# Overflow branch moved in front of the last portion of the expert stream, and the output step behind it in two engines' hands

## Chip, cores and metric

The kernel runs on one core of one Trainium2 chip. The metric is the device time of one launch in microseconds (us); the median of the runs counts.

## What is computed

Two layers of a diffusion backbone over 256 latent tokens and 256 context tokens, 1024 wide. The end of layer 2 is what this change touches: a mixture of eight experts, two per token, then a norm, a gate and the residual.

```python
def moe_swiglu(y, w_r, b_r, wg, wu, wd):
    logits = (y @ w_r).astype(jnp.float32) + b_r.astype(jnp.float32)
    top_val, top_idx = lax.top_k(logits, TOP_K)
    gates = jax.nn.softmax(top_val, axis=-1)
...
    for e in range(N_EXPERTS):
        out = out + combine[..., e:e + 1] * swiglu(y, wg[e], wu[e], wd[e])
    return out
# in the layer:
f = ffn(modulate(rmsnorm(h, g_ffn_pre[i]), sh_f, sc_f))
h = h + gt_f * rmsnorm(f, g_ffn_post[i])
```

## The kernel before

The order of the work is written out while the kernel is built: tasks are Python generators, a planner (`Sched`) picks the next step by estimated times, and each engine gets its instructions in that fixed order. Line 310 is the helper that emits every operation, so nearly all rows carry L310.

The experts' weights, 2 MB each (128 partitions by 4096 floats), come through one queue, SP's, in `t_load` (line 517). Each goes into one of eight big buffers, named `w` in the trace, and a buffer is reused when its last reader is done. An expert's hidden width of 3584 is cut into seven blocks; a block has two transfers for gate and up and one for down, so 6 MB. `moe_items` lists the transfers: block n's gate and up, then block n-1's down.

Tokens are gathered per unit of work. Unit 0 is a fixed expert's, units 1 to 7 are the others by falling load, with room for 160, 96, 96, 64, 64, 64 and 32 tokens (`SLOTS`). `SEQ` gives the order as (unit, first block, block behind the last); its last three entries are unit 7's blocks 2 and 3, then all seven blocks of unit 3 (96 tokens), then unit 7's blocks 4 to 6. `experts` spawns for each entry the gate and up products (`t_xgu`), the down products (`t_xdown`) and the finish (`t_xfinish`: ACT and DVE split the sum in a high and a low part, TensorE spreads it back to the tokens, and DVE adds it to `facc`, the sum over experts, with the token's weight).

Tokens that find no room in their unit go to up to five overflow units, computed only if needed: `moe_over` loads the number of them (`novf`) into a register of every engine, and a nest of five `tc.If` blocks holds the overflow work. That work streams its weights through the same eight buffers, splits them there (ACT and DVE) and multiplies them (TensorE). Each engine runs its own branch when it comes to it in its own order. On the side not taken, each engine waits until its own semaphore (for SP: the eight semaphores of its transfers) has reached the count of everything issued so far, adds what the skipped work would have added, and jumps over the overflow work. The input of these runs has no overflow.

In the kernel before, everything but the last finish comes ahead of the branch. Behind it come that finish (`self.last`) and `fin`: ACT squares `facc` with a running sum, DVE multiplies both token halves (t = 0, 1) by the gate, computes the reciprocal root in ten small operations, and scales and adds the residual in four half tiles, each sent out by SP. `t_gate` builds the gate tile from two groups of TensorE transposes and ACT copies; it waits for a block three before the end of the last entry of `SEQ`.

Of the kernel before, what the change touches and what calls it, by code (L numbers as in the profile page):

```python
# [16 lines left out]
F32 = mybir.dt.float32  # L17
# [4 lines left out]
OP = mybir.AluOpType  # L22
# [4 lines left out]
NE = 8  # L27
FF = 3584
FC = FF // 128
EB = FF // 512  # L30
# [14 lines left out]
MORE = 5  # L45
# [23 lines left out]
POB, HIB = (-1.5, -0.3, -0.8), -0.5  # L69
# [10 lines left out]
PE, ACT, DVE, POOL, DMA, NONE = "PE", "ACT", "DVE", "POOL", "DMA", "NONE"  # L80


def on(eng, *res, ev=()):

    return eng, res, tuple(ev)
# [295 lines left out]
class Core:  # L381
# [196 lines left out]
    def stream(self, items):  # L578


        items = [it if len(it) == 4 else (*it, 1) for it in items]
        for kind, key, ap, n in items:
            for k in [(*key, j) for j in range(4)] if kind[0] == "b" else [key]:
                self.raw[k], self.piece[k], self.uses[k] = Event(), Event(), n
        items = [it[:3] for it in items]
        self.sc.spawn(self.t_load(items))
        self.sc.spawn(self.t_hi(items), HIB)

    def g_proj(self, p, key, c0, c1, kk=2, more=None):

# [1042 lines left out]
        rest = slots - n  # L1633
        return [(s, None) for s in range(0, n, 128)] + ([(n, [64] * (rest // 64) + [32] * (rest % 64 // 32))] if rest else [])

    def experts(self, units, seq):

        go = self.sc.spawn
        prev, state, near = None, {}, []
        for key, b0, b1 in seq:  # L1640
            _, pos, base, slots, comb = units[key]
            down = []
            parts = self.parts(slots)
            for s, ws in parts:
                if b0 == 0:
                    out, hts = [[Event(), Event()], [Event() for _ in ws or [128]]], [Event() for _ in range(EB)]
                    ev = near if prev is None else [*near, *prev] if key >= NE else [*near, *prev, self.combed]
                    go(self.t_xgather(key, pos, base + s, ws, out, ev) if ws else self.t_gather(key, pos, base + s, [out[0], out[1][0]], ev), -0.3)
                    prev = out[0]
                    state[key, s] = out, hts  # L1650
                out, hts = state[key, s]
                if key in JOIN and b0:
                    continue
                d1 = EB if key in JOIN else b1
                acc = [Event() for _ in ws or [128]]
                down.append((self.t_xdown(key, b0, d1, ws, hts, acc) if ws else self.t_edown(key, b0, d1, hts, acc[0]), 0.0))
                for i, w in enumerate(ws or [128]):
                    finish, a = self.t_xfinish if ws else self.t_finish, (comb, acc[i], out[1][i], d1 == EB, *([w] if ws else []))
                    if (key, b0, b1) == seq[-1] and key < NE and (s, ws) == parts[-1] and i == len(ws or [128]) - 1:

                        self.last = lambda done, f=finish, a=a: f(*a, done)
                    else:
                        down.append((finish(*a), -0.2))
            for b in range(b0, b1):
                for s, ws in reversed(parts):
                    out, hts = state[key, s]
                    go(self.t_xgu(key, b, ws, out[0], hts[b]) if ws else self.t_egu(key, b, out[0], hts[b]))
            if self.facc is None:
                self.facc = []
                go(self.t_facc([hts[3]]))  # L1670
            if key not in JOIN:
                near = [hts[max(b0, b1 - NEAR)]]
            if (key, b0, b1) == seq[-1] and key < NE:
                go(self.t_gate([self.colev[1, 5], hts[max(b0, b1 - 3)]]))
            for t in down:
                go(*t)

# [122 lines left out]

    def moe_over(self):

        tc, nc = self.tc, self.nc
        self.sc.settle(KEEP, 3)
        novf = nc.values_load(self.onum[0:1, MORE:MORE + 1], min_val=0, max_val=MORE)
        oidx = [nc.values_load(self.onum[0:1, i:i + 1], engines=(mybir.EngineType.SP,), min_val=0, max_val=NE - 1)
                for i in range(MORE)]

        def more(i):
            with tc.If(novf > i, preferred_fallthrough_block=False):  # L1810
                key = NE + i
                self.stream(self.moe_items([(key, 0, EB)], oidx[i]))
                self.experts({key: (key, lambda: self.otab[:, i, 0:2], 128, 128, lambda: self.otab[:, i, 2:4])}, [(key, 0, EB)])
                self.sc.run()
                if i < MORE - 1:
                    more(i + 1)

        more(0)


    @staticmethod
# [37 lines left out]
    def items(self):  # L1859
        a = self.a  # L1860
        win = lambda i, cs: [("w", ("in", i, c), a["w_in"][i, c]) for c in cs]
        wout = lambda i, s: [("w", ("out", i, s, c), a["w_out"][i, c]) for c in self.wout_order(i, s)]
        ada = lambda i, ch: [("ada", ("ada", i, ch, k), a["w_ada"][i, ch, k]) for k in range(KC)]
        dft = lambda i: [("w", ("dft", i), a["dft"], 2)]
        rest = lambda n: [("rest", None, n)]

        def mix(ws, xs):

            out, n = [], 0
            for j, w in enumerate(ws):  # L1870
                out.append(w)
                m = len(xs) * (j + 1) // len(ws)
                out += xs[n:m]
                n = m
            return out

        x = [("x", t, a["x" if t < 2 else "ctx"][(t % 2) * 128:(t % 2) * 128 + 128, :]) for t in range(4)]
        first = ada(0, 0) + ada(0, 1)
        it = rest(0)
        first[8:8] = win(0, ORD[0][:NW])  # L1880
        for i, w in enumerate(first):
            it += [x[XP.index(i)]] if i in XP else []
            it.append(w)
        m = max(NW, 3)
        it += win(0, ORD[0][NW:m]) + mix(win(0, ORD[0][m:]) + dft(0) + wout(0, 0), mix(sum([ada(0, ch) for ch in (3, 4, 2) if ch not in PA], []), sum([ada(0, ch) for ch in PA], []))) + wout(0, 1)
        ffn = []
        for f in range(FC + 1):
            if f < FC:
                n = 2 if f < NSPLIT else 1
                ffn += [("w", ("gate", f), a["w_gate_d"][f], n), ("w", ("up", f), a["w_up_d"][f], n)]  # L1890
            if f > 0:
                ffn += [("w", ("down", 0, f - 1), a["w_down_d"][f - 1])]
        it += mix(ffn, ada(0, 5) + ada(1, 0) + ada(1, 1) + ada(1, 3) + ada(1, 4))
        it += mix([("w", ("down", 1, f), a["w_down_d"][f]) for f in range(FC)], ada(1, 2) + ada(1, 5))
        it += win(1, ORD[1]) + dft(1)
        moe = self.moe_items(self.seq())
        it += rest(REST1) + moe[:KW] + wout(1, 0) + moe[KW:]
        return it

# [11 lines left out]
    def body(self):  # L1911
        nc, a = self.nc, self.a
# [27 lines left out]
        go = sc.spawn  # L1940
        sc.clock[DMA] = DC
        sc.spawn(self.main())
        sc.run()
        self.moe_over()
        self.fin()

    def main(self):
        go = self.sc.spawn
# [82 lines left out]
        self.sc.rest = REST[0]  # L2031
        self.sc.change, self.sc.stay = CHG, STAY
        tab = lambda u, c: self.tab[:, c:c + 2, 0] if u == 0 else self.utab[:, c:c + 2, u - 1]
        self.experts({u: (u, lambda u=u: tab(u, 0), 0, self.slots(u), lambda u=u: tab(u, 2)) for u in range(NE)}, self.seq())

    def fin(self):

        done = [[Event(), Event()] for _ in range(2)]
        ss = self.fixed([128, 8], F32, "ss", 4)

        def squares():
            junk = yield on(ACT, "h")
# [4 lines left out]
                    self.s.activation(junk, self.facc[t][:, hf * 512:hf * 512 + 512], AF.Square, scale=1.0 / 32.0, accum_out=ss[:, i:i + 1])  # L2047
            self.sc.rel(junk)

        def out(sq):  # L2050
            o = []
            for t in range(2):
                o.append((yield on(DVE, "k", ev=done[t])))
                self.v.tensor_mul(o[t], self.facc[t], self.gate[1, 5, 0].v)
            yield on(DVE, ev=[sq])
            x, t, y = self.fixed([128, 4], F32, "rx", 2), self.fixed([128, 4], F32, "rt", 2), self.fixed([128, 4], F32, "ry", 6)
            self.v.scalar_tensor_tensor(x[:, :2], ss[:, 0:4:2], EPS, ss[:, 1:4:2], op0=OP.add, op1=OP.add)
            self.rsqrt(y[:, :2], x[:, :2], t[:, :2])
            for t in range(2):
                for hf in range(2):  # L2060
                    c = slice(hf * 512, hf * 512 + 512)
                    self.v.scalar_tensor_tensor(o[t][:, c], o[t][:, c], y[:, t:t + 1], self.h[t][:, c], op0=OP.mult, op1=OP.add)
                    self.nc.sync.dma_start(self.out[t * 128:t * 128 + 128, c], o[t][:, c])

        self.sc.spawn(self.last(done))
        self.sc.spawn(out(self.sc.spawn(squares())))
        self.sc.run()


_NAMES = ["x", "ctx", "cc", "consts", "consts2", "dft", "w_ada", "b_ada", "b_cols", "g_cols", "g_mix_post", "g_ffn_post", "w_in",  # L2070
# [98 lines left out]
```

## Time and profile before

| what | us |
|---|---|
| median of 3 runs | 1666.61 (1664.62 to 1667.5) |
| profiled execution | 1667.74 |
| its span, first to last instruction | 1666.0 |
| TensorE busy (matmul) | 1593.7 (96%) |
| DVE, ACT, Pool busy | 786.0, 528.9, 26.1 |

The profile is of one execution. A span of 1666.0 us leaves 1.74 us of its time outside the instructions; this execution was 1.13 us above the median. Times of rows count from the start of the span. PE is TensorE's matmuls, PEld its weight loads, SPq the instructions of SP's queue. Matmuls are pipelined, so a PE that is busy all the time is not a PE at its peak.

### The profile page before, as it was taken

Reading aid. Unit: us, or ns where it says so; the run is one execution under the profiler, and the core shown is the slowest. Engines: PE = TensorE matmul, PEld = TensorE weight load, DVE = VectorE, ACT = ScalarE, POOL = GpSimd, SP = SyncE. Lnnn points to the kernel's source line nnn. Section 1 sums busy time; section 2 is a strip of 40 time slices with the busy share of each in tenths; the row PEclk is TensorE's granted clock in tenths of the full one; section 3 lists DMA queues with packets and bytes.
Section 4 is the critical chain, followed back from the end, with each engine's and each line's share of the span. In section 5 each row is a group of like instructions: output and inputs, shape, how many; then the busy total and the mean of one; then the engine's idle time right before and its main releaser. Section 6 shows DMA issues by size and latency. Waiting matters only on the chain. (4 is left out here: it accounts for less than half of the span.)

```text
span 1666.0 us, 25796 instructions
## 1 busy us (share of the span) xinstructions
PE 1593.7 (96%) x10596; PEld 1029.8 (62%) x10596; DVE 786.0 (47%) x1479; ACT 528.9 (32%) x952; POOL 26.1 (2%) x49
## 2 busy tenths in 40 slices
PE   5999999999999999999998999999999999999995
PEld 3776789888888888897655544444454443343333
DVE  4576688765644448897643342342352421021004
ACT  3477354232322225566613232132132200000001
POOL 0100000000000001000000000000000000000000
PEclk9999999999999999999988999999999999999998
DMA  9515444645554556784499999999999999999994
GB/s 374 214 39 228 164 152 165 214 144 180 170 167 156 174 168 227 259 330 155 152 344 418 421 427 427 426 426 397 427 391 419 427 426 425 425 426 426 426 422 181
DMA packets 71758, 497.30 MB, mean 299 GB/s; under 512 B 9004, under 2 KB 9136, under 8 KB 52048
## 3 DMA queue, kind: packets, MB, share of 16 engines
q1 hardware_dynamic: 68976, 490.76, 74.6%
q0 software_dynamic: 1792, 4.18, 0.8%
q8 instruction: 85, 1.39, 0.3%
q10 hardware_dynamic: 864, 0.62, 0.1%
q14 instruction: 41, 0.34, 0.1%
HBM read 494.49 MB, written 1.05 MB: 297 GB/s over the span
## 5 line engine op out<-in xcount | busy, mean ns | idle before, releaser
L310 PE MATMUL b<-s,s 128*128 128x512 f32 (+2 forms) x2864 | 580.5, 364 | 7.9 <-DVE s L310 6.8
L310 PEld LDWEIGHTS b<-s,s 128*128 128x128 f32 (+1 forms) x2864 | 460.6, 187 | 96.5 <-issue 9.6
L310 PE MATMUL b<-w,f 128*32 128x256 f32 (+1 forms) x2336 | 293.5, 468 | 5.7 <-DMA w<-in_w_gu_e_dram 5.7
L310 PE MATMUL b<-w,s 128*32 128x256 f32 (+2 forms) x1848 | 272.4, 437 | 3.1 <-DMA w<-in_w_gu_e_dram 2.7
L310 DVE TENSOR_TENSOR f<-f,b 128x256 f32<-128x256 f32 (+2 forms) x105 | 41.1, 393 | 480.8 <-ACT f L310 372.3
L310 ACT ACTIVATE f<-b 128x512 f32<-128x512 f32 (+4 forms) x188 | 85.6, 460 | 567.1 <-PE b L310 563.2
L310 PE MATMUL b<-s,f 128*32 128x256 f32 (+1 forms) x1344 | 208.3, 405 | 19.0 <-DVE ones L782 8.6
L310 ACT ACTIVATE s<-s 128x1024 fp32r<-128x1024 f32 (+2 forms) x173 | 179.0, 1050 | 147.2 <-PE b L310 84.0
L310 PEld LDWEIGHTS b<-w,s 128*32 128x32 f32 (+2 forms) x1848 | 152.0, 138 | 117.1 <-issue 72.4
L310 DVE TENSOR_TENSOR s<-s,s 128x1024 fp32r<-128x1024 f32 (+2 forms) x169 | 203.2, 1214 | 31.9 <-ACT s L310 27.9
L310 PEld LDWEIGHTS b<-w,f 128*32 128x32 f32 (+1 forms) x2336 | 103.6, 121 | 167.3 <-issue 130.9
L310 PEld LDWEIGHTS b<-s,f 128*32 128x32 f32 (+1 forms) x1344 | 144.8, 152 | 68.1 <-DMA s<-in_w_ada_dram 12.2
L310 DVE TENSOR_TENSOR w<-w,w 128x1024 fp32r<-128x1024 f32 x84 | 97.2, 1220 | 56.2 <-ACT w L310 56.2
L310 PE MATMUL b<-w,q 128*32 128x256 f32 (+1 forms) x880 | 115.9, 482 | 4.3 <-DMA w<-in_w_down_e_dram 4.3
L310 DVE SCALAR_TENSOR_TENSOR s<-s,cs,s 128x1024 f32<-128x1024 f32 x73 | 91.9, 1280 | 43.4 <-DMA s<-in_w_ada_dram 43.0
L310 ACT ACTIVATE w<-w 128x1024 fp32r<-128x1024 f32 x84 | 81.9, 1046 | 51.1 <-DMA w<-in_w_down_e_dram 27.0
L310 PEld LDWEIGHTS b<-w,q 128*32 128x32 f32 (+1 forms) x880 | 39.7, 123 | 60.7 <-issue 49.4
L310 PEld LDWEIGHTS b<-ident,f 128*128 128x128 f32 x313 | 34.7, 142 | 49.5 <-issue 18.2
L310 DVE SCALAR_TENSOR_TENSOR s<-b,utab,s 128x512 f32<-128x512 f32 (+1 forms) x96 | 52.7, 610 | 24.2 <-PE b L310 24.0
L310 PE MATMUL b<-ident,f 128*128 128x128 f32 x313 | 55.7, 288 | 8.5 <-DVE f L310 4.3
L310 DVE TENSOR_TENSOR s<-b,s 128x512 f32<-128x512 f32 (+2 forms) x67 | 41.7, 625 | 46.5 <-ACT s L310 24.2
L310 ACT ACTIVATE s<-b 128x512 f32<-128x512 f32 (+3 forms) x89 | 44.3, 520 | 35.3 <-PE b L310 33.5
(162 smaller groups left out, 740.7 us busy)
## 6 DMA issues: line engine op xcount, KB each, us to landing
w<-in_w_gu_e_dram SPq DMA_DIRECT2D x101, 2048.0 KB, 17.9
w<-in_w_down_e_dram SPq DMA_DIRECT2D x52, 2048.0 KB, 18.8
s<-in_w_ada_dram SPq DMA_DIRECT2D x96, 512.0 KB, 4.8
s<-in_w_down_d_dram SPq DMA_DIRECT2D x56, 512.0 KB, 4.5
s<-in_w_gu_e_dram SPq DMA_DIRECT2D x44, 512.0 KB, 7.4
s<-in_w_gate_d_dram SPq DMA_DIRECT2D x28, 512.0 KB, 4.7
s<-in_w_up_d_dram SPq DMA_DIRECT2D x28, 512.0 KB, 3.7
s<-in_w_in_dram SPq DMA_DIRECT2D x24, 512.0 KB, 7.0
```

The lines of the kernel that those rows point to most:

```text
L310: r = f(out, *a, **k)
```

## The change

The stream of expert weights is split. The transfers of the last entry of `SEQ` (unit 7, blocks 4 to 6: six for gate and up, three for down, nine in all) leave the main list and become `self.end`. The main part runs all entries but the last; then comes the overflow branch; behind it the last nine transfers are streamed, the last entry's products are computed, and `fin` runs with them in one planner run. The five loads of expert numbers for the overflow work move into the branches. The planner's clocks and free lists are put back to what they were ahead of the branch. The gate tile is built after the first block of the last entry but one (unit 3). In `fin` the gate product of t = 0 goes to Pool, in two halves, that of t = 1 stays on DVE, and the results leave with t = 1 first. `t_hi` isn't spawned for a list without items for it.

```diff
-    def experts(self, units, seq):
+    def experts(self, units, seq, state, whole=((),)):
 
         go = self.sc.spawn
-        prev, state, near = None, {}, []
+        prev, near = None, []
...
-                    if (key, b0, b1) == seq[-1] and key < NE and (s, ws) == parts[-1] and i == len(ws or [128]) - 1:
-
-                        self.last = lambda done, f=finish, a=a: f(*a, done)
-                    else:
-                        down.append((finish(*a), -0.2))
+                    if (key, b0, b1) == whole[-1] and (s, ws) == parts[-1] and i == len(ws or [128]) - 1:
+                        self.fdone = [[Event(), Event()] for _ in range(2)]
+                        a += (self.fdone,)
+                    down.append((finish(*a), -0.2))
...
-            if (key, b0, b1) == seq[-1] and key < NE:
-                go(self.t_gate([self.colev[1, 5], hts[max(b0, b1 - 3)]]))
+            if (key, b0, b1) == whole[max(len(whole) - 2, 0)]:
+                go(self.t_gate([self.colev[1, 5], hts[b0]]))
...
     def moe_over(self):
 
-        tc, nc = self.tc, self.nc
+        tc, nc, sc = self.tc, self.nc, self.sc
+        clock, free = dict(sc.clock), {p: {str(tag): t for t, tag in x} for p, x in sc.free.items() if p != "p"}
         self.sc.settle(KEEP, 3)
         novf = nc.values_load(self.onum[0:1, MORE:MORE + 1], min_val=0, max_val=MORE)
-        oidx = [nc.values_load(self.onum[0:1, i:i + 1], engines=(mybir.EngineType.SP,), min_val=0, max_val=NE - 1)
-                for i in range(MORE)]
 
         def more(i):
             with tc.If(novf > i, preferred_fallthrough_block=False):
                 key = NE + i
-                self.stream(self.moe_items([(key, 0, EB)], oidx[i]))
-                self.experts({key: (key, lambda: self.otab[:, i, 0:2], 128, 128, lambda: self.otab[:, i, 2:4])}, [(key, 0, EB)])
+                idx = nc.values_load(self.onum[0:1, i:i + 1], engines=(mybir.EngineType.SP,), min_val=0, max_val=NE - 1)
+                self.stream(self.moe_items([(key, 0, EB)], idx))
+                self.experts({key: (key, lambda: self.otab[:, i, 0:2], 128, 128, lambda: self.otab[:, i, 2:4])}, [(key, 0, EB)], {})
                 self.sc.run()
                 if i < MORE - 1:
                     more(i + 1)
 
         more(0)
+
+        sc.clock.update(clock)
+        for p, x in free.items():
+            sc.free[p] = sorted(((x.get(str(tag), 0.0), tag) for _, tag in sc.free[p]), key=lambda y: y[0])
+        sc.qrest = 0
...
+        e, b0, _ = self.seq()[-1]
         moe = self.moe_items(self.seq())
+        end = lambda it: it[0] != "rest" and it[1][1] == e and it[1][2] >= b0
+        self.end = [it for it in moe if end(it)]
+        moe = [it for it in moe if not end(it)]
         it += rest(REST1)
...
         self.moe_over()
+        self.stream(self.end)
+        self.experts(*self.units, self.seq()[-1:], *self.state)
         self.fin()
+        sc.run()
...
+        self.units = [{u: (u, lambda u=u: tab(u, 0), 0, self.slots(u), lambda u=u: tab(u, 2)) for u in range(NE)}]
+        self.state = {}, self.seq()
+        self.experts(*self.units, self.seq()[:-1], *self.state)
...
     def fin(self):
 
-        done = [[Event(), Event()] for _ in range(2)]
+        done = self.fdone
         ss = self.fixed([128, 8], F32, "ss", 4)
+        o = [Event(), Event()]
 
         def squares():
             junk = yield on(ACT, "h")
@@ -2047,24 +2062,27 @@
                     self.s.activation(junk, self.facc[t][:, hf * 512:hf * 512 + 512], AF.Square, scale=1.0 / 32.0, accum_out=ss[:, i:i + 1])
             self.sc.rel(junk)
 
+        def gated(t, name, eng):
+            x = yield on(name, "k", ev=done[t])
+            for c in (slice(0, 512), slice(512, 1024)) if name == POOL else (slice(0, 1024),):
+                eng.tensor_mul(x[:, c], self.facc[t][:, c], self.gate[1, 5, 0].v[:, c])
+            self.sc.set(o[t], x)
+
         def out(sq):
-            o = []
-            for t in range(2):
-                o.append((yield on(DVE, "k", ev=done[t])))
-                self.v.tensor_mul(o[t], self.facc[t], self.gate[1, 5, 0].v)
-            yield on(DVE, ev=[sq])
-            x, t, y = self.fixed([128, 4], F32, "rx", 2), self.fixed([128, 4], F32, "rt", 2), self.fixed([128, 4], F32, "ry", 6)
+            yield on(DVE, ev=[sq, o[1]])
+            x, r, y = self.fixed([128, 4], F32, "rx", 2), self.fixed([128, 4], F32, "rt", 2), self.fixed([128, 4], F32, "ry", 6)
             self.v.scalar_tensor_tensor(x[:, :2], ss[:, 0:4:2], EPS, ss[:, 1:4:2], op0=OP.add, op1=OP.add)
-            self.rsqrt(y[:, :2], x[:, :2], t[:, :2])
-            for t in range(2):
+            self.rsqrt(y[:, :2], x[:, :2], r[:, :2])
+            for t in (1, 0):
                 for hf in range(2):
                     c = slice(hf * 512, hf * 512 + 512)
-                    self.v.scalar_tensor_tensor(o[t][:, c], o[t][:, c], y[:, t:t + 1], self.h[t][:, c], op0=OP.mult, op1=OP.add)
-                    self.nc.sync.dma_start(self.out[t * 128:t * 128 + 128, c], o[t][:, c])
-
-        self.sc.spawn(self.last(done))
+                    yield on(DVE, ev=[o[t]])
+                    self.v.scalar_tensor_tensor(o[t].v[:, c], o[t].v[:, c], y[:, t:t + 1], self.h[t][:, c], op0=OP.mult, op1=OP.add)
+                    self.nc.sync.dma_start(self.out[t * 128:t * 128 + 128, c], o[t].v[:, c])
+
+        self.sc.spawn(gated(0, POOL, self.g))
+        self.sc.spawn(gated(1, DVE, self.v))
         self.sc.spawn(out(self.sc.spawn(squares())))
-        self.sc.run()
```

## Rows read from the trace of the kernel before

**Rows 1.** Page, part 2: the span in 40 equal slices of 41.65 us.
```profile
GB/s 374 214 39 228 164 152 165 214 144 180 170 167 156 174 168 227 259 330 155 152 344 418 421 427 427 426 426 397 427 391 419 427 426 425 425 426 426 426 422 181
```

**Rows 2.** Windows of the end: length, busy us (instructions) by engine, PEclk, DMA share, GB/s.
```profile
1560.00:1598.00 38.00, 38.00 (x358) 15.10 (x357) 1.84 (x5) 3.07 (x8) 0.00 (x0) 1.00 1.01 425
1598.00:1643.00 45.00, 44.68 (x507) 19.81 (x500) 7.94 (x18) 3.52 (x10) 0.00 (x0) 1.00 0.92 389
1651.00:1666.00 15.00, 1.23 (x16) 0.96 (x16) 9.77 (x24) 2.89 (x8) 0.00 (x0) 0.50 0.19 72
```

**Rows 3.** Timeline of SP's queue: start, us to the last one's end, instruction, count.
```profile
1618.48 5.78 SPq L517 DMA_DIRECT2D w<-in_w_down_e_dram  x2
```

**Rows 4.** Page, part 6, and line 2063: landing times of weights and of output.
```profile
w<-in_w_down_e_dram SPq DMA_DIRECT2D x52, 2048.0 KB, 18.8
...
DMA to landing us min/median/max: 2.0/2.0/2.1
```

**Rows 5.** Line 1810, the branch: durations ns min/median/max, first and last start; who waited.
```profile
L1810 SPq EVENT_SEMAPHORE  x8: 17/17/17, 1642.8 to 1643.3; - x8
L1810 SPq COMPARE_BRANCH  x2: 43/48/53, 1627.8 to 1643.4; - x2
L1810 PEldq COMPARE_BRANCH  x2: 95/1771/3447, 1646.7 to 1647.8; - x2
L1810 PEldq EVENT_SEMAPHORE  x1: 51/51/51, 1647.7 to 1647.7; - x1
...
  ACT f L310: 3.1, 1
```

**Rows 6.** Line 2063, the output: SP's first own instruction behind the branch.
```profile
L2063 SPq EVENT_SEMAPHORE  x4: 17/17/17, 1646.0 to 1662.5; - x4
```

**Rows 7.** Waits of SP's queue from 1600 us: total us, times, longest.
```profile
SPq L1810 <- SPq L1810: 15.0, 1, 15.0
```

**Rows 8.** Timeline of TensorE's last 108 us: start, us, instruction, shapes, count, idle before.
```profile
1558.10 7.25 PE L310 MATMUL b<-w,s 128*64 128x512 f32 x80 [1.31 <-DMA w<-in_w_gu_e_dram]
...
1604.45 19.44 PE L310 MATMUL b<-w,f 128*32 128x256 f32 x200
...
1624.08 8.97 PE L310 MATMUL b<-w,f 128*32 128x256 f32 x112
...
1634.24 1.16 PE L310 MATMUL b<-ident,cols 128*128 128x128 f32 x8
...
1635.90 1.41 PE L310 MATMUL b<-f,q 64*128 64x512 f32 x20
...
1637.80 1.05 PE L310 MATMUL b<-f,q 64*128 64x512 f32 x4
...
1643.92 3.66 PE L310 MATMUL b<-w,q 128*32 128x256 f32 x64
1651.42 1.23 PE L310 MATMUL b<-f,q 32*128 32x256 f32 x16 [3.83 <-issue]
```

**Rows 9.** Timeline of ACT and DVE, same columns.
```profile
1647.70 0.39 ACT L310 ACTIVATE f<-b 128x256 fp32r<-128x256 f32 x1 [3.07 <-PEq L1810]
1648.12 0.42 DVE L310 TENSOR_TENSOR f<-b,f 128x256 fp32r<-128x256 f32 x1 [5.40 <-ACT f L310]
...
1636.66 5.86 DVE L310 SCALAR_TENSOR_TENSOR s<-b,utab,s 128x512 f32<-128x512 f32 x12 [1.85 <-PE b L310]
...
1652.64 3.22 DVE L310 SCALAR_TENSOR_TENSOR s<-b,utab,s 128x256 f32<-128x256 f32 x8 [4.10 <-PE b L310]
1655.78 2.35 DVE L310 TENSOR_TENSOR s<-s,s 128x1024 f32<-128x1024 f32 x2
```

**Rows 10.** A TensorE pause near 1500 us: timeline, and the window behind its restart (columns as in rows 2).
```profile
1504.07 3.58 PE L310 MATMUL b<-w,q 128*32 128x256 f32 x32 [3.29 <-DMA w<-in_w_down_e_dram]
...
1504.00:1507.60 3.60, 3.53 (x34) 1.84 (x34) 0.00 (x0) 0.00 (x0) 0.00 (x0) 0.53 1.01 428
```

**Rows 11.** Pool's operations by shape: busy us, mean ns of one, idle before.
```profile
L310 POOL CAST s<-f 64x512 fp32r<-64x512 f32 x4 | 2.4, 608 | 0.2
```

More of the change, by code (lines that the diff above doesn't have):

```diff
@@ L586, in stream @@
         self.sc.spawn(self.t_load(items))
-        self.sc.spawn(self.t_hi(items), HIB)
+        if any("w" in it[0] for it in items):
+            self.sc.spawn(self.t_hi(items), HIB)
     def g_proj(self, p, key, c0, c1, kk=2, more=None):
@@ L2033, in main @@
         tab = lambda u, c: self.tab[:, c:c + 2, 0] if u == 0 else self.utab[:, c:c + 2, u - 1]
-        self.experts({u: (u, lambda u=u: tab(u, 0), 0, self.slots(u), lambda u=u: tab(u, 2)) for u in range(NE)}, self.seq())
+        self.units = [{u: (u, lambda u=u: tab(u, 0), 0, self.slots(u), lambda u=u: tab(u, 2)) for u in range(NE)}]
+        self.state = {}, self.seq()
+        self.experts(*self.units, self.seq()[:-1], *self.state)
     def fin(self):
-        done = [[Event(), Event()] for _ in range(2)]
+        done = self.fdone
         ss = self.fixed([128, 8], F32, "ss", 4)
+        o = [Event(), Event()]
         def squares():
```

## Prediction

> **What bounds the kernel now.** I read the slices first: from slice 22 to 39 the transfers run at 418 to 427 GB/s but for two slices, a flat ceiling, and the last slice falls to 181 [rows 1]. So the expert stage is tied to its weights: a 2 MB transfer takes 2.097 MB / 426 GB/s = 4.92 us of the queue. The windows of the end come next: from 1560 to 1643 TensorE is busy too, 38.0 of 38 and 44.7 of 45 us at full clock [rows 2]. The reader is to see two tight resources side by side: TensorE is a little behind in the heavy unit 3, and the eight buffers hold what it hasn't used yet. Then the very end. SP's last weight goes out at 1618.48 + 5.78 - 0.33 = 1623.9 and lands some 18.8 us later, about 1642.7 [rows 3, 4]. TensorE's last product of the down matrix ends at 1647.58 [rows 8]. Then ACT and DVE split it until 1648.54 [rows 9], and TensorE, which could go on at once, starts the last spreading at 1651.42 with an idle time of 3.83 put down to "issue" [rows 8]. That gap is the branch: of its two branch instructions on TensorE one took 95 ns and one, the jump over the overflow work, 3447 ns from 1647.8 [rows 5]. Behind it DVE alone works, 9.8 of 15 us [rows 2].
>
> **Two rows of the branch matter more than its 3.4 us.** SP came to it at 1627.8, left it at 1643.4, and waited 15.0 us in between; its eight semaphore instructions run from 1642.8 to 1643.3, right behind the last landing [rows 5, 7]. So a queue that crosses the branch first lets all its transfers land. And each engine adds the count of the skipped work only when it crosses itself: TensorE at 1647.7, after its last product. The first ACT instruction behind the branch waited 3.1 us and was released by that very step of TensorE [rows 5, 9]. Whatever reuses a buffer of the overflow work waits for that add, since only it tells that the overflow work is through.
>
> **Part 1: nine transfers move behind the branch.** The main part's last transfer is unit 3's last down weight. Counting back from the landing at 1642.8 it lands nine transfers earlier, about 1642.8 - 9 x 4.92 = 1598.5. SP then adds (0.6 us) and jumps: its next own instruction came 2.65 us after the jump, 1646.0 against 1643.4 [rows 5, 6], so it is ready near 1601.8. But the overflow work streams through the same eight buffers, so all of them have their last user inside the branch, as the program stands. Their transfers must wait until TensorE (for a buffer that last held split weights) or DVE (for one that last held raw weights) has crossed. TensorE crosses when all main work is done. When is that? From 1604.45 to 1647.58 TensorE works 43.1 us [rows 8]. Of it, these go behind the branch: per block of unit 7, gate and up are 8 x 4 products of 128*32 and 128x256, recorded twice, so 64 records; the row with 64 of this form took 3.66, hence 3 x 3.66 = 11.0; and a down block is half as many, 3 x 1.83 = 5.5. Two gate groups, 2 x 1.16 = 2.3, go to the front. 43.1 - 16.5 - 2.3 = 24.3 are left, and end at 1628.7. Then unit 3's split is no longer covered: its sums were complete at 1633.05 and the spreading began at 1635.90 [rows 8], 2.85 us that other products filled. And the gate's 2.3 us, now inside unit 3's time, find only 1.31 us of waiting for a landing to fill [rows 8], so 1.0 stays. Bounds 1628.7 (all of that hidden, or the planner fills it) and 1632.5; I take 1632.0, near the upper end, because no other work is left to fill with.
>
> So the queue stands still from 1598.5 to 1632.1. A transfer alone needs 2.0 us to land at 256 KB [rows 4], of which 0.6 is 0.262 MB at 426 GB/s; so 1.4 + 4.9 = 6.3, first landing 1638.4. Eight more at 4.92 give 1677.7, against 1642.8: **+34.9**. Eight of the nine find their buffers free at once, the ninth needs the first one's reader, long done by then.
>
> **Part 2: TensorE behind the last landing.** Before, 4.8 us of work were left there. Now TensorE has been fed at 4.92 us per half block and has only the last down block to do. It costs 1.83 at full clock. It may be more: after a pause of 3.29 us the clock was granted at 0.53 of full, the lower of its two levels (1.2 of 2.4 GHz), and 32 such records took 3.58 instead of half of 3.66 [rows 10]. A portion that waits between landings invites this. Bounds 1.83 and 3.58, I take 2.7 and 0.1 for the start: 1680.5, so with part 1 it is +32.9 at the end of the products.
>
> **Part 3: the gap at the end goes.** From the last product to the first spreading it was 3.84 us, now split and hops, 1647.58 to 1648.54 and two tenths, 1.2: -2.6. The Trainium skill (Advanced Engine Details and Errata, section Control Flow Timing) gives about 108 ns for a compare-and-branch; the rows show 95 ns for one that falls through and 3447 for the one that jumps. By the page this part would be worth 0.1 and the sum 2.5 us higher; the measurement decides. The jumps of ACT, DVE and TensorE now lie in the 6 us before the first landing (TensorE: 1632.0 + 3.5 = 1635.5 against 1638.4), so they cost nothing; if their fetch is slower, 2.9 us are in hand.
>
> **Part 4: the output step.** DVE's two gate products, 2.35 us, stood in the chain [rows 9]. Now one, 1.18, remains; Pool's runs beside the additions to the second half and the root, and its result is asked for last. Nothing in the trace shows Pool at a two-input product; the nearest row is a cast at 608 ns for 512 elements [rows 11]. From the end of the first four additions (half of 3.22) to the first use of t = 0 lie the other four, DVE's product and the root: 1.6 + 1.18 = 2.8 us and more, room for two halves at twice that row. So -1.2, bounds -1.2 and 0 (Pool in DVE's way). The Trainium skill (SBUF — State Buffer, section "SBUF: two separate sides") says that DVE and GpSimd share a port pair under an exclusive lock, which a DVE operation with two SBUF inputs takes against a GpSimd one that reads SBUF. By it DVE's remaining product would wait for a Pool half, and the gain would shrink to about nothing: 1.2 us more in the sum. No row here shows the two side by side.
>
> The five loads that move into the branches stood on SP at 1624 to 1627.7, under its 15 us wait: nothing. The planner's copies cost no device time. The four output transfers only change their order.
>
> **Sum.** 34.9 - 2.0 (4.8 down to 2.8) - 2.6 - 1.2 = **+29.1 us**. On the profiled execution: 1667.74 + 29.1 = 1696.8; on the median: **1695.7**. Its own range: 1628.7 instead of 1632.0 and full clock take 4.2 off, slow clock and no gain from Pool add 2.1: 1691 to 1698.
>
> **Rivals.**
> *DVE opens the gate, not TensorE.* If the first transfer's buffer last held raw weights, it waits for DVE, whose last addition to unit 3's tokens ended at 1642.52, 3.7 us behind the spreading's 1638.85 [rows 8, 9]. For it: SP issues in order, one such buffer at the head is enough. Against: split weights take two buffers for each raw one, so most buffers end with TensorE. 1695.7 + 3.7 = 1699.4.
> *The transfers don't wait for other engines* (on the other side: not slower). If a buffer's last real user in the main part is all that counts, SP goes on at 1601.8. First landing 1608.1, ninth 1647.4, and TensorE's own path decides: crossing at 1632.0, jump 3.5, 16.5 us of work and 1.8 for the clock, 1653.8, +6.2 against 1647.58; less 2.6 and 1.2: +2.4, 1669.0, within 0.2%. If TensorE's work were shorter, the landing would decide: 1647.4 + 0.1 + 1.83 = 1649.3, +1.7 - 3.8 = -2.1, 1664.5. It turns on one point: whether the first weights go out before or after TensorE's add. For it: eight buffers, several free by 1601. Against: ACT's release by TensorE's add. That instruction also needed TensorE's last product, at 1647.58, so the row doesn't settle it alone.
> *It gets faster beyond that:* only if SP didn't let its transfers land; the 15.0 us say it does.
>
> **How the numbers follow.** A measurement here can tell about 0.2% (3.3 us) from no change. Forecast 0.70, DVE 0.14, no waiting for others 0.09, faster 0.02, worse than all 0.05 (a slow clock over the whole portion, fetches in a loaded queue). The range takes the forecast's and DVE's cases and the runs' own spread of 1.4: 1689 to 1704. Faster 0.02, same 0.08, slower 0.90.
>
> **What would show it.** The page's transfer row must have a hole of some 33 us near 1600 to 1633, with TensorE busy until about 1630 and then mostly idle; SP's first issue behind the branch must start within 1 us of TensorE's (or DVE's) add. The last nine landings must be 4.9 apart, the last product end about 3 us behind the last, and the spreading start 1.2 us later. Pool must show two products beside DVE. If SP issues near 1602, part 1 is wrong and the sum collapses to the second rival.

## The result, and the profile after

The changed kernel takes 1696.53 us (median of 4 runs, 1693.34 to 1698.75), the kernel before 1665.61 beside it (1664.26 to 1667.5). The ratio is 1.0183, with a 95% interval of 1.0169 to 1.0198: slower by 31 us. The forecast was 1695.7. The profiled execution after took 1696.29 us, its span 1694.5 against 1666.0. So 28.5 us of span have to be found.

The slices (page, part 2; each is 42.4 us here) answer to [rows 1]. Where transfers ran at 422 to 426 GB/s up to the last slice, the last three slices now move 221, 206 and 267. The first line is TensorE's granted clock in the same slices.

```profile
PEclk9999999999999999999999999999999999999977
...
GB/s 372 206 38 237 166 133 208 181 171 149 180 157 168 170 195 197 319 247 127 283 383 420 426 427 427 426 427 425 380 426 420 426 426 425 425 425 426 221 206 267
```

Next come the waits of SP's queue from 1550 us on, which answer to [rows 7]: total us, times, longest. SP waits 13.0 us for its landings at the branch, 15.0 before. The 34.1 us are new: SP has passed the branch, wants to issue the first of the nine transfers, and DVE's semaphore step at the branch lets it go.

```profile
SPq L517 <- DVEq L1809: 34.1, 1, 34.1
SPq L1809 <- SPq L1809: 13.0, 3, 4.9
```

The branch's own line, now 1809, answers to [rows 5]: durations in ns, first and last start in us.

```profile
L1809 SPq EVENT_SEMAPHORE  x9: 17/17/17, 1579.5 to 1592.9; - x9
L1809 SPq COMPARE_BRANCH  x2: 38/48/57, 1579.4 to 1593.0; - x2
L1809 PEldq COMPARE_BRANCH  x2: 91/1880/3670, 1624.7 to 1625.7; - x2
L1809 DVEq COMPARE_BRANCH  x2: 51/53/55, 1629.2 to 1630.2; - x2
L1809 PEldq EVENT_SEMAPHORE  x1: 51/51/51, 1625.6 to 1625.6; - x1
L1809 DVEq EVENT_SEMAPHORE  x1: 21/21/21, 1630.1 to 1630.1; - x1
```

And SP's timeline from 1570 us on, which answers to [rows 3]. Two lines stand on either side of the hole.

```profile
1576.70 2.06 SPq L517 DMA_DIRECT2D w<-in_w_down_e_dram  x2
1630.30 2.97 SPq L517 DMA_DIRECT2D w<-in_w_gu_e_dram  x4
1633.48 0.33 SPq L517 DMA_DIRECT2D w<-in_w_down_e_dram  x1
1634.01 0.93 SPq L517 DMA_DIRECT2D w<-in_w_gu_e_dram  x2
1635.13 16.88 SPq L517 DMA_DIRECT2D w<-in_w_down_e_dram  x2
```

Read together: SP adds its last count at 1592.9 and jumps. TensorE adds its own at 1625.6, and nothing is issued. DVE adds at 1630.1, and the first issue starts 0.2 us later. The windows around it answer to [rows 2] (length, busy us by engine, PEclk, DMA share, GB/s): 36 us with the queue idle, then a queue that needs three microseconds to come up to speed.

```profile
1594.00:1630.00 36.00, 30.52 (x279) 11.51 (x267) 7.12 (x15) 1.64 (x4) 0.00 (x0) 0.96 0.01 2
...
1631.00:1632.00 1.00, 0.00 (x0) 0.00 (x0) 0.00 (x0) 0.00 (x0) 0.00 (x0) 0.50 0.96 221
1632.00:1633.00 1.00, 0.00 (x0) 0.00 (x0) 0.00 (x0) 0.00 (x0) 0.00 (x0) 0.50 0.88 279
1633.00:1634.00 1.00, 0.00 (x0) 0.00 (x0) 0.00 (x0) 0.00 (x0) 0.00 (x0) 0.50 0.99 410
...
1655.00:1668.00 13.00, 4.61 (x41) 1.96 (x41) 0.29 (x1) 0.28 (x1) 0.00 (x0) 0.50 1.02 432
1668.40:1678.00 9.60, 9.46 (x162) 4.89 (x154) 0.57 (x2) 1.32 (x5) 0.00 (x0) 1.00 0.83 352
```

TensorE's timeline (start, us, instruction, shapes, count, idle before) answers to [rows 8].

```profile
1600.28 0.55 PE L310 MATMUL b<-ident,f 128*128 128x128 f32 x3
...
1622.94 0.50 PE L310 MATMUL b<-f,q 64*128 64x512 f32 x2 [0.76 <-ACT f L310]
1623.67 1.84 PE L310 MATMUL b<-f,q 64*128 64x512 f32 x22 [0.23 <-DVE f L310]
1638.52 1.08 PE L310 MATMUL b<-w,f 128*32 128x256 f32 x8 [13.02 <-DMA w<-in_w_gu_e_dram]
1648.23 4.25 PE L310 MATMUL b<-w,f 128*32 128x256 f32 x48 [8.63 <-DMA w<-in_w_gu_e_dram]
1663.39 4.49 PE L310 MATMUL b<-w,f 128*32 128x256 f32 x40 [10.92 <-DMA w<-in_w_gu_e_dram]
...
1678.39 1.93 PE L310 MATMUL b<-w,q 128*32 128x256 f32 x32 [0.53 <-DMA w<-in_w_down_e_dram]
1680.81 1.09 PE L310 MATMUL b<-f,q 32*128 32x256 f32 x16 [0.49 <-ACT f L310]
```

From the first restart to the start behind the last landing are 39.87 us for eight transfers, 4.98 each: the queue sets the pace, and TensorE idles between landings. The last lines are DVE's timeline, which answers to [rows 9]:

```profile
1624.20 5.86 DVE L310 SCALAR_TENSOR_TENSOR s<-b,utab,s 128x512 f32<-128x512 f32 x12 [0.26 <-PE b L310]
...
1681.92 3.22 DVE L310 SCALAR_TENSOR_TENSOR s<-b,utab,s 128x256 f32<-128x256 f32 x8 [0.70 <-PE b L310]
1685.17 1.47 DVE L310 TENSOR_TENSOR s<-s,s 128x1024 f32<-128x1024 f32 x1
1686.57 0.15 DVE L310 SCALAR_TENSOR_TENSOR rx<-ss 128x2 f32<-128x2 f32 x1
```

and Pool's two products, which had no row before:

```profile
1683.03 2.53 POOL L310 TENSOR_TENSOR s<-s,s 128x512 f32<-128x512 f32 x2 [833.15 <-DVE s L310]
```

The 28.5 us of span, stage by stage along the end of the chain. The last landing moved from 1642.8, where SP's semaphore steps begin [rows 5], to 1678.25 (the chain that ended last has it 0.14 us ahead of the TensorE start that waited for it): +35.5. From there to the end of the last product were 4.8 us, now 1678.39 + 1.93 - 1678.25 = 2.1: -2.7. From that end to DVE's first addition were 1652.64 - 1647.58 = 5.06 us, now 1681.92 - 1680.32 = 1.60: -3.5. From the first addition to the root were 1658.05 - 1652.64 = 5.41 us, now 1686.57 - 1681.92 = 4.65: -0.8. Sum +28.5.

### The profile page after: what moved, and what is told of

Its sections match the earlier page's. It is cut to its first block, busy times and chain, and to the rows that moved or that the text cites. A ratio compares the mean times of both kernels' runs of the same rounds, so it can differ in the third digit from the quotient of the medians.

```text
span 1694.5 us, 25798 instructions
## 1 busy us (share of the span) xinstructions
PE 1593.0 (94%) x10596; PEld 1026.7 (61%) x10596; DVE 785.5 (46%) x1478; ACT 529.1 (31%) x952; POOL 28.7 (2%) x51
## 5 line engine op out<-in xcount | busy, mean ns | idle before, releaser
L310 PE MATMUL b<-w,f 128*32 128x256 f32 (+1 forms) x2336 | 299.7, 479 | 39.7 <-DMA w<-in_w_gu_e_dram 39.7
L310 ACT ACTIVATE f<-b 128x512 f32<-128x512 f32 (+5 forms) x188 | 85.8, 460 | 608.2 <-PE b L310 607.4
L310 DVE TENSOR_TENSOR s<-s,s 128x1024 fp32r<-128x1024 f32 (+1 forms) x168 | 202.3, 1216 | 32.0 <-ACT s L310 27.5
```

Source lines behind the costliest of these rows:

```text
L310: r = f(out, *a, **k)
```

## Experiments

Two theories stood after the result. *The shared buffers:* the nine transfers wait because their buffers were last used, by the program's count, inside the branch, so DVE and TensorE have to cross first. *The rival:* the hole is only SP's own wait for its landings and the way through the branch. The first four kernels are built from the changed kernel.

**No branch.** The call that builds the overflow branch is taken out of the changed kernel.

```diff
-        self.moe_over()
+        sc.settle(KEEP, 0)
```

> The changed kernel without the overflow branch (overflow work is left out; the stream is still in two parts). Theory (all of the loss is the hole that the branch makes in the transfers): no hole, transfers without a pause to 1643 us or so, no jump, the rest as in the changed kernel: against before -3.4 for the gap of the jump, -0.8 for the output step, about -0.3 for the gate net of the uncovered split: 1665.6 - 4.5 = 1661 us (1658 to 1664). Rival (splitting the stream and the new order of TensorE's work cost by themselves): 1670 us or more.

Measured: 1660.55 us, ratio 0.9970 [0.9955, 0.9985] to the kernel before, 1664.98 beside these runs (all ratios are to the kernel before). One line of SP's timeline and one of TensorE's:

```profile
1624.37 5.98 SPq L517 DMA_DIRECT2D w<-in_w_down_e_dram  x2
```

```profile
1627.59 5.39 PE L310 MATMUL b<-w,f 128*32 128x256 f32 x96
```

The hole is gone: SP's last two weights go out from 1624.37 on, and TensorE goes from the spreading, begun at 1625.09, straight into unit 7's products. So the order of work that the change makes is not what costs; the branch in its new place costs all of the 31 us and 5 more.

**Six buffers, five buffers kept out of the branch.** The overflow work gets only the other buffers, so that the first six (five) of the nine transfers have a last user in the main part. The second number of `settle` stands lower, as raw blocks may then use fewer.

```diff
-        self.sc.settle(KEEP, 3)
+        self.sc.settle(KEEP, 1)
+        kept = sc.free["Q"][:6]
+        sc.free["Q"] = sc.free["Q"][6:]
...
         more(0)
 
+        sc.free["Q"] += kept
```

> The changed kernel, but six of the eight weight buffers are kept out of the overflow work, so that only two have a user inside the branch. Theory (a transfer behind the branch waits because its buffer was last used by the overflow work, until DVE and TensorE have added their counts): six transfers go out right behind SP's own crossing, near 1596 us, the last three near 1630 us; landings of those three 1638, 1643 and 1648, last product near 1650 instead of 1680, time 1696.5 - 30 = 1666.5 us (1663 to 1670). Rival (SP's crossing itself or the split of the stream makes the hole, not the buffers): the first issue stays near 1630 us and the time at 1696 us.

> The same with five buffers kept out of the overflow work. Theory: five transfers near 1596 us, four near 1630 us, landings of those at 1638, 1643, 1648 and 1653, so one transfer of 4.9 us later than with six: last product near 1655, time 1671.5 us (1668 to 1675). Rival: no step of 4.9 us between five and six, both at 1696 us.

Measured: six 1669.2 us, ratio 1.0025 [1.0013, 1.0038]; five 1672.98, 1.0055 [1.0034, 1.0075]. SP's timeline with six:

```profile
1599.79 3.19 SPq L517 DMA_DIRECT2D w<-in_w_gu_e_dram  x4
1608.71 0.33 SPq L517 DMA_DIRECT2D w<-in_w_down_e_dram  x1
1614.16 19.34 SPq L517 DMA_DIRECT2D w<-in_w_gu_e_dram  x2
```

SP, which is through the branch, sends what has a free buffer and then waits for DVE at the first that hasn't: of the last line's two, one goes out at 1614.16 and one at 1633.16, behind DVE's step at 1632.9. The six didn't go out near 1596 us as expected, but from 1599.8 to 1614.2: SP's first own instruction comes 2.7 us behind its jump at 1597.0, and for the later ones SP waited until TensorE had read their buffers. The wait for DVE, with six:

```profile
SPq L517 <- DVEq L1811: 18.4, 1, 18.4
```

and with five, where it begins one transfer earlier:

```profile
SPq L517 <- DVEq L1811: 23.8, 1, 23.8
```

The 27 us between six kept buffers and none are what sharing these six cost. That is the first theory, shown; by the rival nothing would have changed. Both times are inside their ranges; six came out 2.7 us above its forecast, and the step from six to five was 3.8 us, put 4.9. With six, 8.6 us against no branch remain, though TensorE waits for no transfer any more. Its timeline shows why:

```profile
1626.49 1.84 PE L310 MATMUL b<-f,q 64*128 64x512 f32 x22 [0.23 <-DVE f L310]
1633.67 8.56 PE L310 MATMUL b<-w,f 128*32 128x256 f32 x96 [5.34 <-DVEq L1811]
```

Two waits end there within half a microsecond. The jump, in the branch's line, took 4845 ns, from 1628.6 to 1633.4; DVE's step at the branch came at 1632.9, and the timeline names it.

```profile
L1811 PEldq COMPARE_BRANCH  x2: 95/2470/4845, 1627.5 to 1628.6; - x2
```

Five kept buffers tell the two apart; the same two views:

```profile
1633.15 5.89 PE L310 MATMUL b<-w,f 128*32 128x256 f32 x56 [4.85 <-DVEq L1811]
```

```profile
L1811 PEldq COMPARE_BRANCH  x2: 95/1960/3825, 1627.5 to 1628.5; - x2
```

That jump was over at 1632.3, and yet TensorE started only at 1633.15, 0.2 us behind DVE's step at 1632.9. So TensorE's own products behind the branch wait for DVE to cross, too, and with six the long jump adds some 0.5 us to that. Then, after a pause of 5.34 us, 96 products took 8.56 us, at a granted clock of 0.50, the lower of the two levels, for the first 3.2 us and 0.66 over the whole stretch, where the kernel without a branch needed 5.39 for the same 96 at 1.00. Between the two profiled executions (spans 1668.0 and 1658.8) the pause is 5.3 us, the slower products 3.2, and 0.7 had come before: 9.2 in all.

**DVE late.** Ahead of the branch DVE gets a memset and eight products on a scratch tile; TensorE's work and the landings are as they were.

```diff
         self.sc.settle(KEEP, 3)
+        x = sc.get(["h"])
+        self.v.memset(x, 0.0)
+        for _ in range(8):
+            self.v.tensor_mul(x, x, x)
+        sc.rel(x)
```

> The changed kernel with nine more operations on DVE (a memset and eight products of 128x512, about 0.69 us each, some 5.8 us) between its last addition of the main part and its branch; they work on a scratch tile. Theory (DVE is the engine whose add opens the gate): SP's wait ends 5.8 us later and the time rises by as much, to 1702.3 us. Rival (TensorE's add opens it; it came at 1625.6 against DVE's 1630.1): SP's first issue and the time stay within 1.5 us.

Measured: 1703.3 us, ratio 1.0240 [1.0217, 1.0263], 7 us above the changed kernel. SP's wait:

```profile
SPq L517 <- DVEq L1814: 39.5, 1, 39.5
```

SP's first issue behind the branch, in its timeline, and TensorE's last spreading ahead of it:

```profile
1637.51 2.65 SPq L517 DMA_DIRECT2D w<-in_w_gu_e_dram  x4
```

```profile
1624.51 1.83 PE L310 MATMUL b<-f,q 64*128 64x512 f32 x22 [0.23 <-DVE f L310]
```

The first issue moved by 7.2 us, from 1630.30 to 1637.51, with TensorE through at 1626.3 (1625.5 in the changed kernel); DVE's nine operations took 6.3 us, and its work before them ended 0.8 later. So it is DVE that opens the gate, and the 7.2 us there came out as 6.8 at the end.

**The other parts by themselves.** From the kernel before: with the early gate tile, with the new output step, with both (the branch in its old place), and, to price the branch there, without a branch (the call `self.moe_over()` is taken out). The edit of the gate tile:

```diff
-            if (key, b0, b1) == seq[-1] and key < NE:
-                go(self.t_gate([self.colev[1, 5], hts[max(b0, b1 - 3)]]))
+            if len(seq) > 1 and (key, b0, b1) == seq[-2]:
+                go(self.t_gate([self.colev[1, 5], hts[b0]]))
```

The output step's edit is `gated` and `out` of the change, and two lines that spawn them:

```diff
+        self.sc.spawn(gated(0, POOL, self.g))
+        self.sc.spawn(gated(1, DVE, self.v))
```

> The kernel before (one stream, branch at its old place ahead of the last finish) with the two other parts of the change: the early gate tile and the output step with one gate product on Pool. Theory (the place of the branch alone makes the change slower; the other parts are gains of their own): -1.3 for the gate (2.3 us out of TensorE's tail, 1.0 back earlier) and -0.8 for the output step: 1665.0 - 2.1 = 1663 us (1661 to 1664.5). Rival (the other parts cost something too, by SBUF slots held longer or by Pool in DVE's way): 1665 us or more.

> The kernel before with the early gate tile alone. Theory: 1665.0 - 1.3 = 1663.7 us; TensorE's two groups of gate transposes leave the last 15 us and stand after unit 3's first block. Rival (TensorE waits for the last landings anyway): no change.

> The kernel before with the new output step alone. Theory: from DVE's first addition of the last finish to the root 4.65 us instead of 5.41, so -0.8: 1664.2 us; DVE's product again near 1.47 us instead of 1.18 because Pool works beside it. Rival (Pool's product is free for DVE): 1.18 us and -1.2.

> The kernel before without the overflow branch (overflow work is left out). Theory (the branch at its old place costs the gap of TensorE's jump, 3.84 us against the 0.5 seen without it): 1665.0 - 3.4 = 1661.6 us. Rival (the jump runs beside work that is needed anyway): 1664 us or more.

Measured, beside 28 runs of the kernel before (median 1665.52 us):

| kernel | us | ratio | interval |
|---|---|---|---|
| both, branch in its old place | 1662.03 | 0.9981 | 0.9971 to 0.9992 |
| early gate tile | 1663.84 | 0.9996 | 0.9984 to 1.0009 |
| new output step | 1664.32 | 0.9990 | 0.9980 to 1.0001 |
| before, without a branch | 1660.21 | 0.9969 | 0.9957 to 0.9982 |

The two small parts together are a gain of 0.2% and beat both kernels; either alone can't be told from nothing. The branch cost 0.3%, some 5 us (by the interval 3 to 7), at its old place, and 36 (1696.53 against 1660.55) at the new one. Of the 5, TensorE's gap explains 3.3: without the branch its last spreading starts after 0.50 us of idle time in place of 3.83.

**What Pool does to DVE.** With Pool's products beside it, DVE's remaining product took 1.42 to 1.49 us, against 2.35 / 2 = 1.18 [rows 9]. Two kernels, both the kernel before with the new output step alone, lengthen what Pool has to do.

```diff
-            for c in (slice(0, 512), slice(512, 1024)) if name == POOL else (slice(0, 1024),):
+            for c in (slice(0, 512), slice(0, 512), slice(512, 1024)) if name == POOL else (slice(0, 1024),):
```

The other one has `(slice(0, 512), slice(0, 1024))` there.

> The kernel before with the new output step alone, and Pool's gate product in three operations of 512 columns, the first half computed twice. Seen so far: Pool's second half overlapped the start of DVE's 128x1024 product by 0.34 to 0.39 us in three kernels, and the product took 1.42 to 1.47 us there against 1.18 without Pool: the overlap less 0.1 us each time. Here Pool's third operation of about 1.25 us follows at once. Theory A, the two engines take turns by whole operations: DVE's product still waits only for the operation that runs when it starts, so it stays at 1.4 to 1.5 us, and Pool's third operation is late or long by about the 1.1 us that DVE then needs. Theory B, both run at once and slow each other down: the product overlaps for its whole length, loses about 0.7 of it, and takes 1.9 to 2.4 us, with Pool's operations at about 1.25 us each. Theory C, Pool doesn't matter to DVE and the product is long for another reason of the new step: 1.42 us, and Pool's third at 1.25 us without a pause. The Trainium skill (SBUF — State Buffer, section SBUF: two separate sides) states a lock of the kind of theory A.

> The kernel before with the new output step alone, and Pool's gate product as one operation of 512 columns (the first half, computed twice) and then one of all 1024. With 1.25 us for 512 columns the second operation runs about 2.5 us from 1.25 us behind Pool's start, so DVE's product finds some 1.6 us of it still to come (0.34 plus 1.25). Theory A, turns by whole operations: the product waits them out, 1.18 + 1.6 - 0.1 = 2.7 us, and the root starts 1.25 us later than with two halves, 5.85 us behind DVE's first addition instead of 4.60. Theory B, both run and slow each other down by the 0.7 of the overlap seen so far: 1.9 to 2.4 us. Theory C, no effect of Pool: 1.42 us and 4.60 us.

Measured by their rows (one execution each, so their times say little). First the new output step as it is, DVE's and Pool's timeline:

```profile
1652.95 1.42 DVE L310 TENSOR_TENSOR s<-s,s 128x1024 f32<-128x1024 f32 x1
1654.29 0.15 DVE L310 SCALAR_TENSOR_TENSOR rx<-ss 128x2 f32<-128x2 f32 x1
...
1650.80 2.49 POOL L310 TENSOR_TENSOR s<-s,s 128x512 f32<-128x512 f32 x2 [800.31 <-DVE s L310]
```

With one long second operation on Pool, the same view:

```profile
1659.12 2.61 DVE L310 TENSOR_TENSOR s<-s,s 128x1024 f32<-128x1024 f32 x1
...
1656.96 3.69 POOL L310 TENSOR_TENSOR s<-s,s 128x512 f32<-128x512 f32 x2 [803.58 <-DVE s L310]
```

With three, the same view:

```profile
1652.24 1.53 DVE L310 TENSOR_TENSOR s<-s,s 128x1024 f32<-128x1024 f32 x1
1653.69 1.21 DVE L310 SCALAR_TENSOR_TENSOR rx<-ss 128x2 f32<-128x2 f32 x1
...
1650.08 4.81 POOL L310 TENSOR_TENSOR s<-s,s 128x512 f32<-128x512 f32 x3 [798.66 <-DVE s L310]
```

Theory A holds. In the first two kernels DVE's product ends 1.08 us after Pool's operation does (1654.37 - 1653.29, 1661.73 - 1660.65), whether 0.34 or 1.53 us of it were left when the product began; in the changed kernel too (1686.64 - 1685.56). With three, Pool's last operation ends at 1654.89 instead of the 1653.9 that three of 1.26 would give: it waited in its turn. DVE's first root operation, two inputs of two columns, behind it took 1.21 us instead of 0.15 and ends with it, at 1654.90. So the engines take turns by whole operations. The Trainium skill (SBUF — State Buffer, section "SBUF: two separate sides") says so, a lock on a shared port pair, and these rows agree with it.

## Why the prediction was right

The time, 1696.53, is within 0.9 us of the forecast. Its steps were not all right, and that closeness is luck: TensorE crossed 6.4 us sooner than put, DVE opened the gate 4.5 us behind it, and the 1.8 us that this left were lost again at the restart of the transfers.

**Right, and shown.** SP lets its transfers land before it jumps (13.0 us). The buffers of the overflow work are what the nine transfers wait for: none kept +31 us, five +9, six +4 by the ratios. The nine then land 4.98 apart (put 4.92). The gap at the end goes: 0.49 us of idle time in place of 3.83. The jumps of all engines hide in the hole: TensorE's, 3670 ns from 1625.7, was over 9 us ahead of the first landing. Two details were off and cost nothing. The hole runs from 1592.9 to 1630.3, put 1598.5 to 1632.1: SP was ready at 1596.0 (1630.1 - 34.1), put 1601.8, and waited all the same. And the ninth transfer found its buffer free only at 1651.68, 16 us after the eighth went out, where I had put "long done by then"; five others were still on their way.

**Wrong: which engine opens the gate.** I put TensorE at 0.70 and DVE at 0.14; it was DVE. My argument, that split weights take two buffers for each raw one, weighs most buffers, while SP issues in order and the first alone decides. DVE's step came 4.5 us behind TensorE's; the rival had put 3.7.

**Wrong: when TensorE crosses.** Put at 1632.0 [bounds 1628.7 to 1632.5], it was 1625.6, outside the bounds. Two terms. The uncovered split was put at 2.85 us and cost 0.76 + 0.23 = 1.0: the spreading can start on the high part as soon as ACT has made it, and only the low part waits for DVE. In the kernel before, other products filled those 2.85 us [rows 8]; they were not the length of the split. The other term: three transposes at 1603.98 in the execution before stand at 1600.28 in this one, although the gate's two groups come earlier in it. That is chance between executions more than the change: the same three stand at 1600.63 to 1606.91 in the five profiled executions with the gate at its old place, and at 1599.13 to 1604.85 in the seven with the early gate. A sum against one profiled execution carries some 3 us either way. These terms, with the 1.0 us put for the gate, make 6.5 of the 6.9 us between the upper bound and the measured 1625.6. Had TensorE opened the gate in this execution, the first issue would have come 4.5 us earlier, and the span would have grown by 24.0 us, 5 under the forecast's 29.1.

So the first issue was at 1630.3, 1.8 us ahead of the 1632.1 put, where rival 1 had 3.7 behind it. The cause is the rival's, the time the forecast's.

**Mis-sized.** *The restart:* first landing 8.1 us after the issue (1638.38), put 6.3. The windows give 221, 279 and 410 GB/s in the first three microseconds; against 426 that is 0.37 MB less, 0.9 us. The rest of the 1.8 isn't divided by any run, but up to that landing the queue moved 337 GB/s for 8.08 us, 2.72 MB, where the transfer has 2.10: bytes of the transfers behind it went ahead of its last ones. The kernel with DVE late shows 205, 197 and 393 and a restart of TensorE 8.4 us after its issue. The length of the pause isn't the cause: with six buffers kept, the queue had stood idle for 2.9 us only (1596.9 to 1599.8), and its first 2 MB landed 8.1 us after the issue as well. *The last down block:* 1.93 us at full clock, put 2.7 for fear of the lower level; TensorE did run at 0.50 in most of the time between landings up to 1668, then had 9.46 us of work in 9.6 at 1.00, and came to the last block at that level. *The gap:* 0.49 us from the end of the last product to the spreading, put 1.2, and 1.60 up to DVE's first addition where the sum had 2.46; again the spreading starts on ACT's part alone. *The output:* -0.8, put -1.2. The bound was named (Pool in DVE's way), the mechanism as the Trainium skill (SBUF — State Buffer, section "SBUF: two separate sides") has it. What was wrong was the price I had put to it, a whole Pool half: the product waits only for what is left of Pool's second operation when DVE comes to it, 0.39 us here, since Pool starts while DVE still adds from PSUM, which doesn't hold it up (3.22 us with Pool beside it, as before).

In sum: -1.8 at the gate, +1.8 in the restart and +0.6 in the eight landings; -0.7 in the last block, -0.9 in the gap, +0.4 in the output: -0.6 us against the forecast's 29.1, which are the 28.5 of the span.

**The price of the jump.** The gap was worth 3.3 us (3.83 to 0.49), as the 3447 ns of [rows 5] said. By the figure of the Trainium skill (Advanced Engine Details and Errata, section Control Flow Timing), about 108 ns for a compare-and-branch, it would have been worth 0.1.

## To carry to other kernels

A conditional block that isn't taken still ties together what its body would have touched: a buffer that the body shares with the stream around it is free only when every engine that uses it there has crossed, so a stream behind the block starts with the slowest of these engines. Work of an engine behind the block can wait in the same way, as TensorE's products did for DVE with five buffers kept. Count what the body shares before you move it to where a stream runs; kept buffers won back 27 of 31 us here, a place behind the last load all of them. And when an order of issue meets a gate, look at the first item in the queue, not at what most items need.

## What the runs showed of the hardware

- A queue that had stood idle for 37 us moved 57, 229, 328 and 360 GB/s in the first four microseconds from its issue, before it was back at 422 to 432; after 43 us (DVE late) 90, 164, 328 and 410, and after 2.9 us (six buffers kept) 106, 147, 328 and 393. The first 2 MB landed 8.1 to 8.3 us after the issue in all three. What makes the start slow wasn't tried.
- TensorE's jump over the skipped work took 3447 ns in the kernel before, and 3367 to 3825 in the nine profiled executions, that one among them, in which the weights' queue stood idle beside it; 4845 in the one where transfers ran beside it (six buffers kept, 217 GB/s over that stretch). SP's, ACT's, DVE's and Pool's branch instructions took 37 to 57 ns. That the transfers are the cause wasn't tried by itself.
- Pool's product of two 128x512 tiles took 1.26 to 1.30 us. It and a DVE product from SBUF exclude each other for whole operations, also when DVE's has only two columns (1.21 us instead of 0.15); DVE's additions from PSUM run beside it undisturbed.
